# Gathering the seven products of w_up and w_down in shared PSUM tiles, forming the activation sums in the up stage, and 30 instead of 22 column blocks of w_down as sevens

## The chip, the cores and the metric

The kernel runs on one core of a Trainium2 chip. Times are device microseconds (us) of one execution. Before the change three runs took 2043.04, 2046.28 and 2048.93 us; the median is 2046.28 us. Engines are named as in the profile: PE is TensorE, PEld its weight loads, DVE VectorE, ACT ScalarE, POOL GpSimd, SP the engine that issues most DMAs.

## The reference, cut to what matters

A decoder layer on 512 tokens with 16 meta tokens in front: RMSNorm, one input projection, windowed attention beside an mLSTM, an output projection with residual; then the part that the change touches, a squared-ReLU MLP with D_MODEL = 2048 and D_FF = 8192, and a final norm.

```python
u = rmsnorm(h, norm_mlp[l])
h = h + jnp.square(jax.nn.relu(u @ w_up[l])) @ w_down[l]
...
h = rmsnorm(h, norm_final)
```

## The kernel before, in words

All large products are float32 work done as three passes of TensorE: each operand is split into a high part (a ScalarE copy that rounds to float32r, L116) and a low part (a VectorE subtraction, L117), and hi x hi, hi x lo and lo x hi are added up in PSUM. `split` (L115) does one operand; `hi_lo` (L122) gives weight operands from three rotating pairs of tiles `whi`, `wlo` of 128 x 1024. So a weight operand can be made at most two products ahead of TensorE: the third waits until a product has freed its pair.

The MLP is stored and multiplied as 2 x 2 blocks with Winograd's seven products in place of eight. Three stages follow each other.

**Output projection** (up to 711 us). It makes the operands of the seven products for w_up, `yh` and `yl` for p = 0 to 6, partly in pool b2 in the order of `ORDER` (L44), partly in the slots s0 to s31 (`xslot`).

**Up stage** (711 to 1354 us). 32 quads, `up_quad` (L734). A quad loads two raw tiles of 1 MB with blocks x11, x12, x22, x21, forms four sums s1 to s4 on VectorE (`w_sum`, L731, 128 x 1024 each), makes seven weight operands and runs seven products of 24 matmuls with 256 columns (L754 to 756). The products go into four PSUM tiles of their own (pa, pb, pc, pd; odd quads use the second set of four banks). When all are done they are gathered: a copy of the first (L795) and five VectorE adds (L796 to L800) give the four result blocks `d`; Relu and Square on ScalarE (L803, L804) and one store of 512 KB on ACT's queue into `fdram[quad]` (L805) follow. The last quad does it on VectorE and POOL's queue.

**Down stage** (1354 us to the end). The 8192 rows are cut into NC = 8 chunks; each chunk has four column blocks of 512. The activations of a chunk come back from `fdram` (`f_load`, L935: 512 KB a load), and are split into units (`f_unit`, L922): four plain ones, f = 0, 1, 7, 3, and four of sums, f = 2, 4, 5, 6, for which `f_sums` (L950) first does four VectorE operations of 128 x 512 per pair. Plain units are double buffered (slots for even chunks, tiles r for odd ones), the slots of the sums are single: a chunk's sums can only be written once the chunk before has used its own. A column block is done in one of two ways:

- `down_seven` (L997): two raw loads of 1 MB with y11|y21 and y22|y12, four sums, seven products of 24 matmuls with 256 columns (L1012 to 1014) in seven PSUM tiles, then a copy (L1031) and six VectorE adds (L1036 to L1042) into d.
- `down_classic` (L978): two raw loads, four weight operands, 96 matmuls with 512 columns (L706 to 708) from the plain units alone.

`add_block` (L967) and `classic_done` (L991) scale each quarter on ScalarE and add it to `hd` in memory with an accumulating DMA on POOL's queue. Blocks 0 and 1 of each chunk and block 2 of chunks 1 to 6 are sevens, 22 in all; block 3, and block 2 of chunks 0 and 7, are classic, 10 in all, the very last of them token by token with the final norm (after L1091). In each chunk the plain units of the next one are prepared behind its second seven, and the sums while its classic block runs (L1053 to L1066). Raw loads rotate through two `raw_tile`s and one tile of pool b3f (`raw3`, L962).

The order on each engine and queue is not written out: the program is built with `schedule_with_timeline_sim=True` (L1203), where a planner orders the instructions by the place in the program and by when it holds their inputs and tiles to be ready; each engine then runs its queue in that order, and semaphores for tiles and PSUM banks are added by the framework.

Of the kernel before, what the change touches and what calls it, by code (L numbers as in the profile page):

```python
# [10 lines left out]
F32 = mybir.dt.float32  # L11
# [32 lines left out]
ORDER = (0, 1, 3, 4, 6, 5, 2)  # L44
# [38 lines left out]
def hybrid_layer(ctx, tc, io, out):  # L83
# [98 lines left out]
    groups = [(0, 1), (1, 1)] + [(k, 2) for k in range(2, KT, 2)]  # L182
    with tc.tile_pool(name="a0", bufs=1) as a0:
# [511 lines left out]
    fdram = [dpool.tile([P, 4 * HTOK], F32, name=f"fd{i}") for i in range(NQ)]  # L695
# [38 lines left out]
    def up_quad(quad):  # L734
# [12 lines left out]
        pa, pb, pc = (nb((P, 2, HTOK)) for _ in range(3))  # L747
        pd = nb((P, HTOK))

        def product(p, w, out, q0=0, q1=KQ):  # L750
            for q in range(q0, q1):
                wh, wl = (t[:, q * P : (q + 1) * P] for t in w)
                ah_, al_ = yh[p, q // 2][:, q % 2], yl[p, q // 2][:, q % 2]
                pe.matmul(out, wh, ah_, start=q == 0, stop=False)  # L754
                pe.matmul(out, wh, al_, start=False, stop=False)  # L755
                pe.matmul(out, wl, ah_, start=False, stop=q == KQ - 1)  # L756

        pp2, pp6 = pa[:, 1], pd[:]
        if quad == 0:
            pp2, pp6 = pp6, pp2  # L760
# [16 lines left out]
            product(5, operand(s2[:]), pp6)  # L777
        else:
            product(0, operand(x11), pa[:, 0])
            product(1, operand(x12), pp2)  # L780
            product(3, operand(x22), pc[:, 0])
            w_sum(s1, x21, x22, ALU.add)
            w_sum(s2, s1[:], x11, ALU.subtract)
            product(4, operand(s1[:]), pb[:, 1])
            w_sum(s3, x11, x21, ALU.subtract)
            product(6, operand(s3[:]), pb[:, 0])
            w_sum(s4, x12, s2[:], ALU.subtract)
            product(5, operand(s2[:]), pp6)
            product(2, operand(s4[:]), pc[:, 1])

        d = b2b.tile([P, 4, HTOK], F32, name="d", bufs=2)
        sb = b2b.tile([P, HTOK], F32, name="sb")
        u2 = b2b.tile([P, 1, HTOK], F32, name="u2")
        u = b2b.tile([P, 2, HTOK], F32, name="u")
# [412 lines left out]
```

## Time and profile before

| what | before |
|---|---|
| median of 3 runs | 2046.28 us (2043.04 to 2048.93) |
| span of the profiled execution | 2042.5 us |
| median less span | 3.8 us |
| TensorE busy, matmuls | 2010.7 us, 14208 |
| VectorE, ScalarE busy | 1425.2 us, 964.5 us |
| DMA traffic | 284.44 MB, mean 139 GB/s |

The profiler gives the span of its one execution, 2042.5 us, and no other time for it; what lies around the span is taken as the median of the runs less the span. In the tables by stretch, a row has the stretch, its length, the busy time and count of PE, PEld, DVE, ACT and POOL, the granted TensorE clock as a share of full speed, the mean busy share of the 16 DMA engines, and GB/s. In the groups of instructions a row has line, engine, operation, tiles out<-in, shapes and count, then busy us and mean ns of one, then the engine's idle time before them with what ended it. In the waits a row has who waited for whom, us in total, times and the longest.

### The profile page before, as it was taken

How to read it: one execution, taken by the hardware profiler on the slowest of the kernel's cores; microseconds unless marked ns; L12 is line 12 of the kernel's file. 1: busy time of each engine (PE TensorE's matmuls, PEld its weight loads, DVE VectorE, ACT ScalarE, POOL GpSimd, SP SyncE). 2: the span in 40 equal slices, each digit the busy share in tenths (PEclk: the TensorE clock that was granted, in tenths of full speed). 3: DMA queues.
4: the chain of work that ended last, by engine and by line, in shares of the span. 5: the costliest groups of instructions: out<-in, count | busy, mean ns of one | idle time of the engine just before them, and what ended most of it. 6: DMA issues, size and time to landing. Idle time of an engine off the chain costs nothing.

```text
span 2042.5 us, 34088 instructions
## 1 busy us (share of the span) xinstructions
PE 2010.7 (98%) x14208; PEld 1865.8 (91%) x14208; DVE 1425.2 (70%) x1916; ACT 964.5 (47%) x1378; POOL 198.3 (10%) x295
## 2 busy tenths in 40 slices
PE   9999999999999999999999999999999999999998
PEld 7878889988888899999999999988989999899996
DVE  6556763233544587778777877779787897988874
ACT  4433542244433454444444444445555555655553
POOL 0111220012120000000000000001211111211200
PEclk9999999999999999999999999999999999999999
DMA  7412122211433353434334343436665866756762
GB/s 306 137 54 85 63 65 102 83 62 64 139 128 130 118 182 108 155 106 153 119 141 136 123 154 105 155 136 194 176 175 133 218 179 173 180 152 185 196 205 95
DMA packets 72507, 284.44 MB, mean 139 GB/s; under 512 B 11520, under 2 KB 15744, under 8 KB 49168
## 3 DMA queue, kind: packets, MB, share of 16 engines
q1 hardware_dynamic: 50032, 232.96, 33.1%
q0 software_dynamic: 16560, 30.94, 9.2%
q10 hardware_dynamic: 5760, 18.36, 2.2%
q8 instruction: 111, 1.82, 0.4%
q14 instruction: 44, 0.36, 0.1%
HBM read 227.67 MB, written 54.56 MB: 138 GB/s over the span
## 4 chain that ended last, share of the span: by engine, by line
PE 86%; DVE 5%; DMA 5%; ACT 2%; issue 1%; POOL 0%; DVEq 0%; POOLq 0%; SPq 0%; ACTq 0%
PE g L163 10%; PE a L754 5%; PE a L756 5%; PE a L755 5%; PE g L754 5%; PE g L756 5%; PE g L755 5%; PE g L706 4%; PE g L708 4%; PE g L707 4%; DMA raw<-in_w4w_dram 4%; PE g L1013 2%; PE g L1014 2%; PE g L178 2%; PE g L225 2%; PE g L1012 2%
## 5 line engine op out<-in xcount | busy, mean ns | idle before, releaser
L116 ACT CAST whi<-raw 128x1024 fp32r<-128x1024 f32 x294 | 308.5, 1050 | 525.1 <-PE g L708 120.7
L117 DVE TENSOR_TENSOR wlo<-raw,whi 128x1024 fp32r<-128x1024 f32 x294 | 359.4, 1223 | 198.0 <-ACT whi L116 192.5
L117 DVE TENSOR_TENSOR wlo<-s,whi 128x1024 fp32r<-128x1024 f32 x216 | 263.9, 1224 | 106.6 <-ACT whi L116 106.2
L116 ACT CAST whi<-s 128x1024 fp32r<-128x1024 f32 x216 | 226.3, 1048 | 235.3 <-PE a L755 75.3
L163 PE MATMUL g<-s,whi 128*128 128x264 f32 x1216 | 205.0, 287 | 0.2 <-DVE qa L261 0.2
L163 PEld LDWEIGHTS g<-s,whi 128*128 128x128 f32 x1216 | 170.9, 189 | 5.4 <-issue 4.9
L1012 PE MATMUL g<-whi,s 128*128 128x256 f32 x496 | 137.6, 279 | 2.7 <-ACT whi L116 2.7
L1013 PE MATMUL g<-wlo,s 128*128 128x256 f32 x496 | 138.8, 281 | 1.1 <-DVE wlo L117 1.1
L1013 PE MATMUL a<-wlo,s 128*128 128x256 f32 x472 | 132.7, 282 | 6.7 <-DVE wlo L117 6.7
L1014 PE MATMUL g<-whi,s 128*128 128x256 f32 x496 | 138.6, 280 | 0.0
L707 PE MATMUL g<-wlo,s 128*128 128x512 f32 x352 | 138.4, 393 | 0.0
L708 PE MATMUL g<-whi,s 128*128 128x512 f32 x352 | 138.1, 395 | 0.0
L706 PE MATMUL g<-whi,s 128*128 128x512 f32 x352 | 136.7, 396 | 0.1
L1014 PE MATMUL a<-whi,s 128*128 128x256 f32 x472 | 131.8, 280 | 0.0
L1012 PE MATMUL a<-whi,s 128*128 128x256 f32 x472 | 130.5, 280 | 1.1 <-ACT whi L116 1.1
L163 PE MATMUL g<-s,wlo 128*128 128x264 f32 x608 | 128.0, 287 | 0.0
L754 PE MATMUL g<-yh,whi 128*128 128x256 f32 x448 | 126.6, 283 | 1.1 <-ACT whi L116 1.1
L756 PE MATMUL a<-yh,wlo 128*128 128x256 f32 x448 | 126.4, 282 | 0.6 <-DVE wlo L117 0.6
L756 PE MATMUL g<-yh,wlo 128*128 128x256 f32 x448 | 126.3, 282 | 0.0
L754 PE MATMUL a<-yh,whi 128*128 128x256 f32 x448 | 126.3, 282 | 0.0
L754 PE MATMUL a<-s,whi 128*128 128x256 f32 x448 | 126.2, 282 | 0.0
L755 PE MATMUL g<-yl,whi 128*128 128x256 f32 x448 | 126.1, 282 | 0.0
(375 smaller groups left out, 5640.4 us busy)
## 6 DMA issues: line engine op xcount, KB each, us to landing
raw<-in_w_dram SPq DMA_DIRECT2D x112, 1024.0 KB, 5.4
raw<-in_w4w_dram SPq DMA_DIRECT2D x44, 1024.0 KB, 6.8
hd<-d POOLq DMA_DIRECT2D x112, 256.0 KB, 7.9
raw<-in_w4c_dram SPq DMA_DIRECT2D x20, 1024.0 KB, 6.6
fd<-d ACTq DMA_DIRECT2D x31, 512.0 KB, 6.5
fr<-fd SPq DMA_DIRECT2D x28, 512.0 KB, 4.9
xtok<-in_x_dram SPq DMA_DIRECT2D x4, 1024.0 KB, 11.3
hs<-in_x_dram SPq DMA_DIRECT2D x16, 256.0 KB, 6.4
```

The costliest lines, as they stand in the source:

```text
L116: act.copy(dst_hi, src)
L117: dve.tensor_tensor(out=dst_lo, in0=src, in1=dst_hi.bitcast(F32), op=ALU.subtract)
L163: pe.matmul(ps[s][:], w, x[:, s * HALF : (s + 1) * HALF], start=first and kt == 0, stop=last and kt == KT - 1,)
L706: pe.matmul(ps[b][:], a, wh, start=kt == first, stop=False)
L707: pe.matmul(ps[b][:], a, wl, start=False, stop=False)
L708: pe.matmul(ps[b][:], c, wh, start=False, stop=kt == last)
L754: pe.matmul(out, wh, ah_, start=q == 0, stop=False)
L755: pe.matmul(out, wh, al_, start=False, stop=False)
L756: pe.matmul(out, wl, ah_, start=False, stop=q == KQ - 1)
L1012: pe.matmul(ps[p][:, t], a, wh[:, cols], start=q == 0, stop=False)
L1013: pe.matmul(ps[p][:, t], a, wl[:, cols], start=False, stop=False)
L1014: pe.matmul(ps[p][:, t], a2, wh[:, cols], start=False, stop=q == FQ - 1)
```

## The change

The first quad still gathers from four PSUM tiles. Every other quad of the up stage uses three accumulators in two PSUM tiles: X, and W and Q in one bank. Product 0 goes into X and is copied out by ScalarE; products 5, 6 and 3 are added to X in turn, with a copy of X ("snapshot") after 5 and after 6; 1 goes into W, 4 into Q, is copied, and 2 is added to Q. Three VectorE adds finish the blocks. The products run in the order 0, 1, 5, 4, 6, 2, 3, and ORDER follows it. After Square, four more VectorE operations form the sums of the activations, and two stores of 512 KB per quad go out on ACT's queue, with 1 KB pieces side by side for a pair of quads.

In the down stage `f_load`, `f_plain` and `f_sums` are gone: each unit is loaded by itself (256 KB, SP's queue, five buffers `fu`) and split; unit 7 is loaded for chunks 0 and 7 alone. The sevens use X, W and Q in three banks in the same way. All blocks but (chunk 0, block 3) and the last one are sevens. The raw tiles hold y11|y12 and y21|y22, and pool b3f has two raw buffers. The next chunk's plain units 0, 1, 3 are prepared behind block 1, its sums behind block 3. The input arrays `w4c` and `w4w` are laid out to match.

```diff
-ORDER = (0, 1, 3, 4, 6, 5, 2)
+ORDER = (0, 1, 5, 4, 6, 2, 3)
...
+    fdram = [[dpool.tile([P, 4, 2, HTOK], F32, name=f"fd{i}_{n}") for n in range(2)] for i in range(NQ // 2)]
...
+        def product(p, w, out, q0=0, q1=KQ, start=True):
             for q in range(q0, q1):
                 wh, wl = (t[:, q * P : (q + 1) * P] for t in w)
                 ah_, al_ = yh[p, q // 2][:, q % 2], yl[p, q // 2][:, q % 2]
-                pe.matmul(out, wh, ah_, start=q == 0, stop=False)
-                pe.matmul(out, wh, al_, start=False, stop=False)
-                pe.matmul(out, wl, ah_, start=False, stop=q == KQ - 1)
-
-        pp2, pp6 = pa[:, 1], pd[:]
+                pe.matmul(out, wh, ah_, start=start and q == 0, stop=False, skip_group_check=True)
+                pe.matmul(out, wh, al_, start=False, stop=False, skip_group_check=True)
+                pe.matmul(out, wl, ah_, start=False, stop=q == KQ - 1, skip_group_check=True)
...
+            X, B = nb((P, HTOK)), nb((P, 2, HTOK))
+            W, Q = B[:, 0], B[:, 1]
+            d = b2b.tile([P, 4, HTOK], F32, name="d", bufs=2)
+            product(0, operand(x11), X[:])
+            act.copy(d[:, 0], X[:])
             w_sum(s1, x21, x22, ALU.add)
             w_sum(s2, s1[:], x11, ALU.subtract)
+            product(1, operand(x12), W)
+            product(5, operand(s2[:]), X[:], start=False)
+            dve.tensor_tensor(out=d[:, 0], in0=d[:, 0], in1=W, op=ALU.add)
+            act.copy(d[:, 2], X[:])
+            product(4, operand(s1[:]), Q)
             w_sum(s3, x11, x21, ALU.subtract)
+            act.copy(d[:, 1], Q)
+            product(6, operand(s3[:]), X[:], start=False)
             w_sum(s4, x12, s2[:], ALU.subtract)
+            act.copy(d[:, 3], X[:])
+            product(2, operand(s4[:]), Q, start=False)
+            dve.tensor_tensor(out=d[:, 3], in0=d[:, 3], in1=d[:, 1], op=ALU.add)
+            act.activation(d[:, 0], d[:, 0], AF.Relu)
+            product(3, operand(x22), X[:], start=False)
+            dve.tensor_tensor(out=d[:, 2], in0=d[:, 2], in1=Q, op=ALU.add)
+            act.activation(d[:, 2:4], d[:, 2:4], AF.Relu)
+            act.activation(d[:, 1], X[:], AF.Relu)
+        act.activation(d[:], d[:], AF.Square)
+        fs = b2b.tile([P, 4, HTOK], F32, name="fs")
+        dve.tensor_tensor(out=fs[:, 0], in0=d[:, 2], in1=d[:, 3], op=ALU.add)
+        dve.tensor_tensor(out=fs[:, 1], in0=fs[:, 0], in1=d[:, 0], op=ALU.subtract)
+        dve.tensor_tensor(out=fs[:, 2], in0=d[:, 2], in1=d[:, 0], op=ALU.subtract)
+        dve.tensor_tensor(out=fs[:, 3], in0=d[:, 1], in1=fs[:, 1], op=ALU.subtract)
+        act.dma_start(out=fdram[quad // 2][0][:, :, quad % 2], in_=d[:])
+        act.dma_start(out=fdram[quad // 2][1][:, :, quad % 2], in_=fs[:])
...
-        split(hi[:], lo[:], src)
...
-    def f_sums(c, pair):
-        a11, a12, a21, a22 = (frs[c, pair][:, :, i] for i in range(4))
-        s1, s2 = (b3.tile([P, 2, HTOK], F32, name=f"fs{i}")[:] for i in range(2))
-        dve.tensor_tensor(out=s1, in0=a21, in1=a22, op=ALU.add)
-        dve.tensor_tensor(out=s2, in0=s1, in1=a11, op=ALU.subtract)
-        dve.tensor_tensor(out=a12, in0=a12, in1=s2, op=ALU.subtract)
-        dve.tensor_tensor(out=a21, in0=a11, in1=a21, op=ALU.subtract)
-        for f, src in ((2, a12), (4, s1), (5, s2), (6, a21)):
-            f_unit(c, pair, f, src)
...
+        pos = FPOS.index(f)
+        fu = b3f.tile([P, 2, HTOK], F32, name="fu", bufs=5)
+        sync.dma_start(out=fu[:], in_=fdram[2 * c + pair][pos // 4][:, pos % 4])
+        split(hi[:], lo[:], fu[:])
+
+    def prepare(c, fs):
+        for f in fs:
+            for pair in range(2):
+                f_unit(c, pair, f)
 
     raws_ = iter(range(1, 1 << 20))
 
     def raw3(src):
-        raw = raw_tile() if next(raws_) % 3 < 2 else b3f.tile([P, 2048], F32, name="raw3")
+        raw = raw_tile() if next(raws_) % 4 < 2 else b3f.tile([P, 2048], F32, name="raw3", bufs=2)
...
+        y11, y12 = raws[0][:, :1024], raws[0][:, 1024:]
+        y21, y22 = raws[1][:, :1024], raws[1][:, 1024:]
...
+        X, W, Q = bank((P, 2, HTOK)), abank((P, 2, HTOK)), abank((P, 2, HTOK))
+        d = b3.tile([P, NB, 512], F32, name="d", bufs=2)
+
+        def product(p, w, out, start=True):
...
+                    last = t == 1 and q == FQ - 1
+                    pe.matmul(out[:, t], a, wh[:, cols], start=start and t == q == 0, stop=False, skip_group_check=True)
+                    pe.matmul(out[:, t], a, wl[:, cols], start=False, stop=False, skip_group_check=True)
+                    pe.matmul(out[:, t], a2, wh[:, cols], start=False, stop=last, skip_group_check=True)
+
+        def c_out(row, col):
+            return d[:, 2 * row : 2 * row + 2, col * HTOK : (col + 1) * HTOK]
+
+        product(0, operand(y11), X)
+        act.copy(c_out(0, 0), X[:])
         w_sum(t1, y12, y11, ALU.subtract)
         w_sum(t2, y22, t1[:], ALU.subtract)
+        product(1, operand(y21), W)
+        product(5, operand(t2[:]), X, start=False)
+        dve.tensor_tensor(out=c_out(0, 0), in0=c_out(0, 0), in1=W[:], op=ALU.add)
+        act.copy(c_out(0, 1), X[:])
+        w_sum(t3, y12, y22, ALU.subtract)
+        product(4, operand(t1[:]), Q)
+        act.copy(c_out(1, 0), Q[:])
         w_sum(t4, y21, t2[:], ALU.subtract)
+        product(6, operand(t3[:]), X, start=False)
+        act.copy(c_out(1, 1), X[:])
+        product(2, operand(y22), Q, start=False)
+        dve.tensor_tensor(out=c_out(1, 1), in0=c_out(1, 1), in1=c_out(1, 0), op=ALU.add)
+        product(3, operand(t4[:]), X, start=False)
+        dve.tensor_tensor(out=c_out(0, 1), in0=c_out(0, 1), in1=Q[:], op=ALU.add)
+        act.copy(c_out(1, 0), X[:])
...
-    prepare(0, f_plain)
+    prepare(0, PLAIN)
+    down_classic(0, 3, classic_done)
+    prepare(0, (5, 4, 6, 2))
     for c in range(NC - 1):
-        if c == 0:
-            down_classic(c, 3, classic_done)
-            prepare(c, f_sums)
-        down_seven(c, 0, add_block)
-        down_seven(c, 1, add_block)
-        prepare(c + 1, f_plain)
-        if c == 0:
-            down_classic(c, 2, classic_done)
-        else:
-            down_seven(c, 2, add_block)
-            down_classic(c, 3, classic_done)
-        prepare(c + 1, f_sums)
+        for j in range(3 if c == 0 else 4):
+            down_seven(c, j, add_block)
+            if j == 1:
+                prepare(c + 1, (0, 1, 3))
+        prepare(c + 1, (5, 4, 6, 2))
+        if c == NC - 2:
+            prepare(c + 1, (7,))
...
-    down_classic(c, 2, last_done)
+    down_seven(c, 2, last_done)
```

## Rows read from the trace of the kernel before

**Rows 1.** The page's first part: span; busy time by engine.

```profile
span 2042.5 us, 34088 instructions
...
PE 2010.7 (98%) x14208; PEld 1865.8 (91%) x14208; DVE 1425.2 (70%) x1916; ACT 964.5 (47%) x1378; POOL 198.3 (10%) x295
```

**Rows 2.** Busy time by stretch: up stage, then three stretches of the down stage.

```profile
771.00:1334.00 563.00, 563.00 (x4738) 563.00 (x4737) 444.98 (x455) 268.93 (x283) 0.00 (x0) 1.00 0.38 132
1354.20:1445.30 91.10, 85.38 (x530) 75.83 (x529) 81.65 (x104) 52.06 (x74) 11.87 (x14) 1.00 0.63 179
...
1697.40:1781.50 84.10, 81.50 (x602) 77.10 (x602) 70.66 (x83) 46.73 (x61) 13.95 (x17) 1.00 0.67 176
...
1476.00:1496.00 20.00, 16.96 (x130) 16.75 (x129) 13.97 (x16) 7.21 (x9) 0.57 (x1) 0.91 0.42 117
```

**Rows 3.** Timeline of PE at four borders between classic blocks and sevens.

```profile
1593.91 0.63 PE L706 MATMUL a<-whi,s 128*128 128x512 f32 x2
...
1616.12 0.40 PE L1012 MATMUL g<-whi,r 128*128 128x256 f32 x2
...
1675.66 0.63 PE L706 MATMUL a<-whi,r 128*128 128x512 f32 x2
...
1697.44 0.40 PE L1012 MATMUL g<-whi,s 128*128 128x256 f32 x2
```

**Rows 4.** Waits of PE in the down stage, 1354.2 to 2043 us.

```profile
PE a L1013 <- DVE wlo L117: 9.7, 7, 3.0
PE g L1013 <- DVE wlo L117: 3.4, 4, 1.6
PE g L1012 <- ACT whi L116: 2.7, 1, 2.7
PE a L1012 <- ACT whi L116: 1.1, 1, 1.1
```

**Rows 5.** The chain that ended last, 1465 to 1490 us: start us, us, what.

```profile
1474.69 8.34 DMA raw<-in_w4w_dram
...
1487.25 1.15 DVE wlo L117
```

**Rows 6.** Groups of instructions by shape, DVE, 1400 to 1990 us.

```profile
L117 DVE TENSOR_TENSOR wlo<-raw,whi 128x1024 fp32r<-128x1024 f32 x93 | 113.3, 1220 | 17.7 <-ACT whi L116 17.4
...
L732 DVE TENSOR_TENSOR s<-raw,s 128x1024 f32<-128x1024 f32 x42 | 51.3, 1221 | 0.4
L117 DVE TENSOR_TENSOR s<-fr,s 128x512 fp32r<-128x512 f32 x52 | 35.1, 686 | 5.0 <-ACT s L116 5.0
...
L953 DVE TENSOR_TENSOR fs<-fr 128x512 f32<-128x512 f32 x13 | 8.9, 686 | 0.1
...
L1036 DVE TENSOR_TENSOR d<-sb,g 128x512 f32<-128x512 f32 x11 | 7.5, 680 | 0.0
```

**Rows 7.** Groups of instructions by shape, ACT, 1400 to 1990 us.

```profile
L116 ACT CAST whi<-raw 128x1024 fp32r<-128x1024 f32 x92 | 96.7, 1052 | 120.4 <-PE a L1014 41.9 <-PE g L1014 35.8 <-PE g L708 23.5
...
L969 ACT ACTIVATE d<-d,r 128x512 f32<-128x512 f32 x80 | 52.8, 715 | 22.8 <-DVE d L1042 18.7 <-DVE d L1040 4.1
L116 ACT CAST s<-fr 128x512 fp32r<-128x512 f32 x52 | 31.9, 619 | 17.5 <-DMA fr<-fd 4.4 <-PE g L1013 3.6 <-DVE fr L955 3.6
...
L1031 ACT COPY sb<-g 128x512 f32<-128x512 f32 x11 | 6.4, 578 | 0.0
```

**Rows 8.** Waits in the up stage, 771 to 1334 us.

```profile
ACT whi L116 <- PE a L755: 145.8, 84, 1.8
ACT whi L116 <- PE g L755: 144.4, 83, 2.0
```

**Rows 9.** Groups of instructions by shape in the up stage, ACT and DVE.

```profile
L795 ACT COPY sb<-g 128x256 f32<-128x256 f32 x14 | 5.1, 363 | 0.0
...
L796 DVE TENSOR_TENSOR d<-sb,g 128x256 f32<-128x256 f32 x14 | 5.8, 414 | 0.0
```

**Rows 10.** The page's DMA issues: count, KB each, us to landing.

```profile
fd<-d ACTq DMA_DIRECT2D x31, 512.0 KB, 6.5
```

More of the change, by code (lines that the diff above doesn't have):

```diff
@@ L694, in hybrid_layer @@
     hd = [[dpool.tile([P, 512], F32, name=f"hd{j}_{b}") for b in range(NB)] for j in range(NJ)]
-    fdram = [dpool.tile([P, 4 * HTOK], F32, name=f"fd{i}") for i in range(NQ)]
+    NC = 8
+    fdram = [[dpool.tile([P, 4, 2, HTOK], F32, name=f"fd{i}_{n}") for n in range(2)] for i in range(NQ // 2)]
     ssh = cpool.tile([P, NB, NJ], F32, name="ssh")
@@ L777, in up_quad @@
             product(5, operand(s2[:]), pp6)
-        else:
-            product(0, operand(x11), pa[:, 0])
-            product(1, operand(x12), pp2)
-            product(3, operand(x22), pc[:, 0])
+            d = b2b.tile([P, 4, HTOK], F32, name="d", bufs=2)
+            v = b2b.tile([P, 4, HTOK], F32, name="fs")
+            sb, u2, u = v[:, 2], v[:, 3], v[:, :2]
+            act.copy(sb, pa[:, 0])
+            dve.tensor_tensor(out=d[:, 0], in0=sb, in1=pp2, op=ALU.add)
+            dve.tensor_tensor(out=u2, in0=sb, in1=pp6, op=ALU.add)
@@ new lines, in up_quad @@
+            dve.tensor_tensor(out=u, in0=v[:, 3:].to_broadcast([P, 2, HTOK]), in1=pb[:], op=ALU.add)
+            dve.tensor_tensor(out=d[:, 3], in0=u[:, 0], in1=pb[:, 1], op=ALU.add)
+            dve.tensor_tensor(out=d[:, 1:3], in0=u, in1=pc[:], op=ALU.add)
+            act.activation(d[:], d[:], AF.Relu)
+        else:
+            X, B = nb((P, HTOK)), nb((P, 2, HTOK))
+            W, Q = B[:, 0], B[:, 1]
+            d = b2b.tile([P, 4, HTOK], F32, name="d", bufs=2)
+            product(0, operand(x11), X[:])
+            act.copy(d[:, 0], X[:])
@@ L787, in up_quad @@
+            product(6, operand(s3[:]), X[:], start=False)
             w_sum(s4, x12, s2[:], ALU.subtract)
[L788 to L794, printed above, removed]
-        act.copy(sb[:], pa[:, 0])
-        dve.tensor_tensor(out=d[:, 0], in0=sb[:], in1=pp2, op=ALU.add)
@@ L1022, in down_seven @@
-        w_sum(t3, y22, y12, ALU.subtract)
-        product(5, operand(t2[:]))
-        w_sum(t4, y21, t2[:], ALU.subtract)
-        product(6, operand(t3[:]))
-        product(3, operand(t4[:]))
-        d = b3.tile([P, NB, 512], F32, name="d", bufs=2)
-        sb = b3.tile([P, 2, HTOK], F32, name="sb")
-        u0, u1 = (b3.tile([P, 2, HTOK], F32, name=f"u{i}") for i in range(2))
-        act.copy(sb[:], ps[0][:])
-        def c_out(row, col):
-            return d[:, 2 * row : 2 * row + 2, col * HTOK : (col + 1) * HTOK]
```

80 lines of the change are left out of this document (13 added, 67 removed).

## The prediction

> **What bounds the kernel now.** I read the page first: TensorE is busy for 2010.7 us of a span of 2042.5 us, so only what shortens its stream or its gaps can move the end [rows 1]. A busy share of matmuls says little about their pace, so I read paces next, in the table by stretch. In the up stage 4738 matmuls of 256 columns fill 563 us without a gap, 0.119 us each, with the full clock granted; VectorE is busy for 79% of it and ScalarE for 48% [rows 2]. In the down stage the timeline gives clean blocks: a classic block of 96 matmuls of 512 columns runs from 1593.91 to 1616.12 (22.21 us), the next from 1675.66 to 1697.44 (21.78 us), and the 504 matmuls between, three sevens, take 59.54 us, 19.85 us each [rows 3]. So a seven is 2.15 us shorter than a classic block (mean 22.0 us), and one product of 24 matmuls lasts 2.84 us.
>
> Third, the waits. In the up stage before, TensorE waits for nothing. In the down stage it waits 16.9 us in all: 13.1 us for the low half of a weight operand, 3.8 us for a high half [rows 4]. The chain shows what stands behind them: a load of w_down lands late, VectorE forms the sums and the low half late, TensorE idles [rows 5]. VectorE is the busy helper there (70.66 of 84.1 us in one chunk of the down stage, 84%, against 46.73 us for ScalarE) [rows 2].
>
> **The change part by part.** The sum is made against the profiled span of 2042.5 us. The median of the runs is 3.8 us longer (2046.28 us); I add that at the end.
>
> *Eight more blocks as sevens.* Before, 10 of 32 blocks of w_down are classic (one of them the token by token end); afterwards 2. 8 x (22.0 - 19.85) = **-17.2 us**, on TensorE itself, so nothing hides it; this term is only lost if a wait eats it. [...]
>
> *Four raw buffers, and other halves side by side.* A load of w_down now has two b3f buffers beside the two raw tiles (before one), and a pair holds y11|y12 and y21|y22, so the first sum needs the first load alone. The waits with the chain of rows 5 should go: two whole blocks fit, and a load can start 20 us ahead, where it took 8.34 us and came late. Bounds: -16.9 us (all TensorE waits) and 0. I take **-8 us**, about half, because VectorE stays nearly full, as follows.
>
> *VectorE in the down stage.* A seven has 7 low halves and 4 sums of 1.22 us, and 6 adds of 0.68 us; afterwards 3 such adds. Per chunk before: 3 x 17.5 + a classic block's 4 low halves (4.9) + 16 unit splits (11.0) + 8 sum operations (5.5) = 73.9 us, against 59.55 + 22.0 = 81.6 us of TensorE. Afterwards: 4 x 15.5 + 14 x 0.687 = 71.6 us against 4 x 19.85 = 79.4 us [rows 6]. So 90% as before; the sum operations leave, but the classic block, in which VectorE caught up, leaves too. What used to be done under it (the splits of the activation sums, whose slots are single) must now follow the products: each pair of slots comes free when the last seven of the chunk has used it and is needed seven products later, six products or 17 us of cover. Cost 0; if that cover goes, each late pair is 2 x 0.69 us on the path.
>
> *Snapshots.* One PSUM tile X now takes products 0, 5, 6 and 3 in turn, with a ScalarE copy after each of the first three; a second (Q) takes 4 and then 2. Each copy must finish within the one product between: 2.84 us. No row shows such a copy between two products; the nearest are the copies at the end of a seven, 0.363 us (256 columns) and 0.578 us (512) [rows 7, 9]. In front of one can stand a weight cast of 1.05 us that is already running: 1.6 us together, inside 2.84. In the up stage ScalarE waits for TensorE 290 us of 563 [rows 8], so it is free when a product ends: cost 0; the cover is that wait. There W and Q also share one bank, so product 4 waits for VectorE's add of W; product 5 lies between. In the down stage ScalarE rises from 3 x 10.8 + 7.1 + 9.9 = 49.4 us a chunk to 4 x (7.35 + 2.89 + 2.86) + 14 x 0.618 = 61.0 us of 79.4 (60% to 77%) [rows 7]. In the last seven of a chunk, copy, weight cast and two unit casts make 2.87 us against 2.84, and the product with two scalings as well 3.7. That is about 1.1 us late per chunk, 7.7 us over seven chunks if no operand made ahead absorbs it; I take half, **+4 us**. Bounds 0 (a copy cannot shorten the stream) and the price under the second rival.
>
> *Activation sums in the up stage.* Per quad VectorE has four adds of 256 columns more (0.41 us each [rows 9]) and two of 512 fewer (0.69 us [rows 6]), 15.8 to about 16.1 us of 20; ScalarE gains three copies and a Relu in three pieces, 1.5 us, to 11 of 20. TensorE waits for neither now [rows 2], so nothing can be gained. One store of 512 KB more per quad, issued by ScalarE behind VectorE's last subtraction: what is queued behind it are weight casts, which run two products ahead, and it lands in about 6.5 us [rows 10] of the 20 us that its single tile has. The stretch's DMA share rises from 0.38 to some 0.46. Cost 0; the upper bound is ScalarE's extra work on the path, 1.5 us x 31 quads = 46 us, which needs its 290 us of waiting gone, and is counted with the second rival. On SP's queue, 30 reads of 512 KB become 116 of 256 KB, ahead of or behind weight loads; a chunk then moves about 206 GB/s against 176, share 0.78 against 0.67 [rows 2]. Cost 0 as long as four raw buffers keep loads a block ahead. POOL's queue loses its three transfers and keeps the accumulating stores.
>
> *The end.* The last seven (7,2) stands where a classic block left the slots of the sums free for 22 us. Now the eight splits of the last weights (0.62 + 0.69 us each) follow that block's products, the last two pairs one product before use: 0 to 8 x 0.69 = 5.5 us, **+2 us**. The start of the stage keeps its classic block as cover; 0.
>
> Sum: -17.2 - 8 + 4 + 2 = -19.2 us; 2023.3 us of span, **2027 us** of time.
>
> **The rivals.** *All waits go.* The extra raw buffer is all that was missing, as three sevens in a row without a wait suggest [rows 3]: -17.2 - 16.9 = -34 us, 2012 us. Against it: VectorE at 90%.
>
> *A late snapshot, the slower end.* In the down stage a copy is queued behind a weight cast that itself waits for the end of the product between, or for a sum that VectorE has not formed. Then TensorE idles for that cast and the copy, 1.05 + 0.58 = 1.63 us. There are 4 such places in each of 61 sevens. If one in every seven of the down stage is late, 30 x 1.63 = 49 us: 2027 + 49 = **2076 us**. It decides from 12 late copies on (19.2 / 1.63) of 244. For it: each engine runs its queue in order, the order is a planner's and not the source's, and ScalarE has at most 2.84 us. Against: the copy stands earlier in the program than the casts it competes with, and those wait for the same product's end. [...] The clock would join in only at longer waits: a stretch with one of 3.0 us was granted 0.91, the start of the stage with waits up to 2.7 us 1.00 [rows 2, 4].
>
> *VectorE becomes the bound.* If a chunk keeps the 84.1 us that one takes now [rows 2], because VectorE's idle share (16%) stays whatever the blocks are, the shorter stream turns into waits: 71.6 / 0.84 = 85 us a chunk, **2046 us**, no change. For: 90%. Against: part of the idle time is the load wait that goes.
>
> **How the numbers follow.** Forecast (2014 to 2040) 0.65, all waits go 0.10, VectorE bound 0.09, late snapshots 0.16. About 0.3% (6 us) is what a measurement tells from no change, so faster 0.75, same 0.09, slower 0.16. The range 2008 to 2052 takes in the first three and the lightest of the fourth (a late copy in half of the down sevens gives 2051).
>
> **What would show it.** Right: 5040 matmuls of the sevens at about 0.118 us; no TensorE wait in the up stage; fewer waits for low halves with w_down loads behind them; a chunk near 80 us. Wrong: TensorE waits whose releaser is a ScalarE copy out of X or Q, repeated per seven; a chunk above 82 us; a gap before the last columns above 5 us; an up stage longer than 20 us a quad.

## The result, and the profile after

The changed kernel takes 2033.14 us (median; 2032.67 to 2035.11) against 2045.14 us for the kernel before on the same chip: a ratio of 0.9938, 95% interval 0.9923 to 0.9953, so 12.0 us faster. The profiled execution spans 2033.3 us against 2042.5. The forecast was 2027 us, in a range of 2008 to 2052.

In the code after, the up products are L753 to L755, the classic ones L707 to L709, the sevens L1009 to L1011. ScalarE's snapshots are L1017 (X after product 0), L1023 (X after 5), L1026 (Q after 4) and L1029 (X after 6), the last copy L1034, the scalings by r2 L964; a unit is loaded at L947 and cast at L116.

First the page's busy times, to set against [rows 1]:

```profile
span 2033.3 us, 35953 instructions
...
PE 1993.5 (98%) x14784; PEld 1878.7 (92%) x14784; DVE 1397.5 (69%) x1897; ACT 1083.4 (53%) x1675; POOL 199.5 (10%) x292
```

The table by stretch (columns as in [rows 2]): the up stage, the first classic block with the wait ahead of it, its first part alone, and chunks 1 to 6 from the first matmul of chunk 1 to that of chunk 7.

```profile
771.00:1334.00 563.00, 563.00 (x4738) 563.00 (x4738) 435.63 (x508) 301.97 (x422) 0.00 (x0) 1.00 0.46 158
...
1357.20:1383.80 26.60, 24.44 (x100) 19.27 (x99) 18.23 (x25) 13.58 (x21) 0.00 (x0) 0.94 0.86 274
...
1357.20:1365.00 7.80, 5.64 (x18) 4.03 (x17) 5.58 (x10) 5.09 (x8) 0.00 (x0) 0.78 0.86 292
...
1446.40:1938.00 491.60, 476.85 (x4034) 474.62 (x4034) 402.07 (x420) 339.35 (x468) 84.74 (x96) 1.00 0.79 205
```

The up stage holds the same 4738 matmuls in the same 563 us. Ahead of that stretch, in the second quad, TensorE has four waits, with L800 the add of W:

```profile
PE a L753 <- DVE d L800: 0.8, 1, 0.8
PE a L753 <- ACT whi L116: 0.6, 2, 0.3
PE a L755 <- DVE wlo L117: 0.6, 1, 0.6
```

Chunks 1 to 6 are 24 sevens, 24 x 19.85 = 476.4 us at the pace of [rows 3]; they take 491.6, so 15.2 us are lost there. What is lost, the waits of PE from 1357 us to the end show, against [rows 4]:

```profile
PE g L1009 <- ACT d L1017: 16.9, 8, 2.8
PE g L1009 <- ACT d L1029: 2.8, 5, 0.6
PE g L707 <- ACT s L116: 2.1, 1, 2.1
PE g L1009 <- ACT d L989: 0.4, 1, 0.4
```

In the down stage no wait for a low half (DVE wlo) or a weight cast (ACT whi) is left. In their place product 5 waits for the snapshot of product 0, once in the first seven of each of the eight chunks. The timeline of ACT at such a border (start, us, what, idle before), and the matmul that waited, in the timeline of PE:

```profile
1447.44 1.97 ACT L116 CAST s<-fu 128x512 fp32r<-128x512 f32 x3 [2.46 <-DMA fu<-fd]
1449.32 0.58 ACT L1034 COPY d<-g 128x512 f32<-128x512 f32 x1
1449.80 1.05 ACT L116 CAST whi<-s 128x1024 fp32r<-128x1024 f32 x1
1450.75 0.62 ACT L116 CAST s<-fu 128x512 fp32r<-128x512 f32 x1
1451.27 2.57 ACT L964 ACTIVATE d<-d,r 128x512 f32<-128x512 f32 x4
1453.73 0.61 ACT L116 CAST s<-fu 128x512 fp32r<-128x512 f32 x1
1454.24 0.58 ACT L1017 COPY d<-g 128x512 f32<-128x512 f32 x1
```

```profile
1454.88 0.39 PE L1009 MATMUL g<-whi,s 128*128 128x256 f32 x1 [2.51 <-ACT d L1017]
```

ScalarE first stands 2.46 us for a unit's landing, then works off what piled up: five unit casts, a copy, a weight cast and four scalings stand ahead of the snapshot. Eight sum-unit casts of the next chunk, and six plain casts of the chunk after it, all come here: fourteen in some 25 us (at the last border it is the eight and two of unit 7). Plain units have slots of their own and are not needed for 80 us; the planner puts them ahead of their place in the source, where they stand behind block 1 of the next chunk.

### The profile page after: what moved, and what is told of

The parts are those of the page before. It is cut to its first block, busy times and chain, and to the rows that moved or that the text cites. A ratio compares the mean times of both kernels' runs of the same rounds, so it can differ in the third digit from the quotient of the medians.

```text
span 2033.3 us, 35953 instructions
## 1 busy us (share of the span) xinstructions
PE 1993.5 (98%) x14784; PEld 1878.7 (92%) x14784; DVE 1397.5 (69%) x1897; ACT 1083.4 (53%) x1675; POOL 199.5 (10%) x292
## 4 chain that ended last, share of the span: by engine, by line
PE 89%; DMA 4%; ACT 3%; DVE 3%; issue 1%; POOL 1%; POOLq 0%; DVEq 0%; ACTq 0%
PE g L163 9%; PE a L753 5%; PE a L755 5%; PE g L753 5%; PE g L755 5%; PE a L754 5%; PE g L754 5%; PE g L1009 5%; PE g L1011 5%; PE g L1010 5%; DMA fu<-fd 3%; PE a L1010 3%; PE a L1011 3%; PE a L1009 3%; PE g L707 3%; PE g L709 3%
## 5 line engine op out<-in xcount | busy, mean ns | idle before, releaser
L116 ACT CAST whi<-raw 128x1024 fp32r<-128x1024 f32 x286 | 300.9, 1052 | 406.4 <-PE g L709 91.3
L117 DVE TENSOR_TENSOR wlo<-raw,whi 128x1024 fp32r<-128x1024 f32 x286 | 350.0, 1224 | 207.1 <-ACT whi L116 201.7
L117 DVE TENSOR_TENSOR wlo<-s,whi 128x1024 fp32r<-128x1024 f32 x248 | 302.4, 1223 | 140.8 <-ACT whi L116 137.7
L116 ACT CAST whi<-s 128x1024 fp32r<-128x1024 f32 x248 | 260.8, 1053 | 157.0 <-PE g L754 64.5
L1009 PE MATMUL g<-whi,s 128*128 128x256 f32 x720 | 201.5, 280 | 18.9 <-ACT d L1017 16.9
L1010 PE MATMUL g<-wlo,s 128*128 128x256 f32 x720 | 201.6, 280 | 0.0
L1011 PE MATMUL g<-whi,s 128*128 128x256 f32 x720 | 201.4, 280 | 0.0
L1010 PE MATMUL a<-wlo,s 128*128 128x256 f32 x600 | 167.6, 279 | 0.0
L1011 PE MATMUL a<-whi,s 128*128 128x256 f32 x600 | 167.6, 279 | 0.0
L1009 PE MATMUL a<-whi,s 128*128 128x256 f32 x600 | 166.7, 278 | 0.0
L1009 PEld LDWEIGHTS g<-whi,s 128*128 128x128 f32 x720 | 135.0, 188 | 21.3 <-ACT d L1017 18.5
L965 POOL DMA_DIRECT2D hd<-d x108 | 95.3, 1115 | 461.9 <-ACT d L964 461.9
L1011 PEld LDWEIGHTS g<-whi,s 128*128 128x128 f32 x720 | 136.5, 190 | 0.0
L1010 PEld LDWEIGHTS g<-wlo,s 128*128 128x128 f32 x720 | 135.2, 188 | 0.0
L753 PE MATMUL a<-yh,whi 128*128 128x256 f32 x448 | 126.5, 282 | 1.5 <-DVE d L800 0.8
L753 PE MATMUL g<-yh,whi 128*128 128x256 f32 x448 | 126.6, 282 | 1.1 <-ACT whi L116 1.1
L755 PE MATMUL a<-yh,wlo 128*128 128x256 f32 x448 | 126.4, 282 | 0.6 <-DVE wlo L117 0.6
L755 PE MATMUL g<-yh,wlo 128*128 128x256 f32 x448 | 126.2, 282 | 0.0
L753 PE MATMUL a<-s,whi 128*128 128x256 f32 x448 | 126.1, 282 | 0.0
```

The lines of the kernel that those rows point to most:

```text
L116: act.copy(dst_hi, src)
L117: dve.tensor_tensor(out=dst_lo, in0=src, in1=dst_hi.bitcast(F32), op=ALU.subtract)
L753: pe.matmul(out, wh, ah_, start=start and q == 0, stop=False, skip_group_check=True)
L755: pe.matmul(out, wl, ah_, start=False, stop=q == KQ - 1, skip_group_check=True)
L965: pool.dma_start(out=hd[j][b][:], in_=d[:, b], accum_op=ALU.add)
L1009: pe.matmul(out[:, t], a, wh[:, cols], start=start and t == q == 0, stop=False, skip_group_check=True)
```

## The experiments

Each time is a median with the ratio to the kernel before on the same chip. "Chunks 1 to 6" is, for each run, the stretch from the first matmul of chunk 1 to that of chunk 7: the same 4032 matmuls, 476.4 us without a loss.

**Why the snapshot is late: landing, queue order, or the snapshot itself.** The first four runs: three try a remedy that turns out wrong, the fourth undoes the gather. nf (the weights of the final norm) moves into a raw3 tile where the added tiles need its place.

```diff
# e1_fu9
-        fu = b3f.tile([P, 2, HTOK], F32, name="fu", bufs=5)
+        fu = b3f.tile([P, 2, HTOK], F32, name="fu", bufs=9)
...
-    nf = b3f.tile([P, D], F32, name="nf")[:]
+    nf = b3f.tile([P, 2048], F32, name="raw3", bufs=2)[:]
```

> Nine buffers fu for unit loads instead of five (the final norm weights take a raw tile to make room; chunk 7 then has three raw tiles). Theory L, landing: the late copy after product 0 at the head of each chunk (eight TensorE waits, 16.9 us) starts with ScalarE idle in front of a unit cast whose load could not be issued for want of a buffer; with nine the cast never waits for DMA, ScalarE is 2 to 3 us earlier, at least six of the eight waits go, and the time is 2017 to 2023 us against 2033. Theory Q, queue: the copy is late because four scalings and unit casts stand in front of it; the waits shrink only by what the DMA wait was, and 2026 to 2031 us remain. Theory F, ScalarE simply full: no change, 2031 to 2035 us.

Measured: 2048.99 us, ratio 1.0008 (0.9999 to 1.0018), some 15 us slower than the change and above all three ranges. Chunks 1 to 6 take 504.0 us. The waits of PE in the down stage, and the timeline of ACT at the border:

```profile
PE g L1009 <- ACT d L1023: 9.7, 6, 2.7
PE g L1009 <- ACT d L1017: 6.9, 5, 1.7
PE g L1009 <- ACT whi L116: 4.5, 6, 1.7
PE g L1010 <- DVE wlo L117: 3.8, 6, 0.8
```

```profile
1434.08 1.66 ACT L116 CAST s<-fu 128x512 fp32r<-128x512 f32 x3 [4.05 <-DMA fu<-fd]
...
1439.55 2.18 ACT L116 CAST s<-fu 128x512 fp32r<-128x512 f32 x4
```

With more buffers the planner puts more casts in a row, at the borders up to four where the change has up to three, and they still run into a landing: more buffers did not take the landing away. What makes this kernel slower than the change was not isolated; 12.4 of the 15 us are lost in chunks 1 to 6, and 3.3 in chunk 7 (65.3 us against 62.0), where nf holds a raw buffer.

```diff
# e2_defer
         product(0, operand(y11), X)
         act.copy(c_out(0, 0), X[:])
+        flush()
...
-        done(c, j, d)
+        held.append((done, c, j, d))
...
```

> The four scalings and stores of a seven are written down behind the next seven's first copy, everything else as in the change. Theory Q: the planner now puts the copy after product 0 in front of the scalings, the eight waits go and the time is 2015 to 2021 us. Theory L: the copy still stands behind a unit cast that waits for its load; waits shrink by the 2.6 us of the scalings where the load lands in time and stay where it does not, 2020 to 2029 us. Theory F: the scalings are done later and some other copy is late instead, 2031 to 2035 us.

Measured: 2034.82 us, ratio 0.9947 (0.9934 to 0.9960), the change's own time. The trace is of an execution of 2041.5 us. The scalings are written behind the next seven's snapshot, but ScalarE's timeline still has the four of them ahead of it, at 1453.62 us (the snapshot, now L1024, runs at 1456.59): the planner's order is not the source's. So this run does not test what the scalings cost. The wait stays:

```profile
PE g L1016 <- ACT d L1024: 16.3, 7, 3.0
```

e3_both makes both edits.

> Both edits: nine unit buffers, and the scalings written behind the next seven's first copy. Theories L and Q: no snapshot wait above 1 us is left, 2013 to 2020 us; if one of the two alone was the cause, the same time as that run within 3 us. Theory F: TensorE still waits for ScalarE about 15 us in the down stage, 2028 us or more.

Measured: 2051.49 us, ratio 1.0016 (1.0003 to 1.0030): like e1_fu9.

```diff
# e4_banks: the gather undone, one of seven banks for each product
-        product(0, operand(y11), X)
-        act.copy(c_out(0, 0), X[:])
+        product(0, operand(y11))
...
+        act.copy(sb[:], ps[0][:])
+        dve.tensor_tensor(out=c_out(0, 0), in0=sb[:], in1=ps[1][:], op=ALU.add)
...
```

> The sevens of w_down gather as before the change, seven PSUM tiles, one copy and six VectorE adds at the end; up stage, stored sums, four raw buffers and 30 sevens stay (the final norm weights take a raw tile). Theory S: the waits are the price of the snapshots, so the eight waits on the copy vanish; VectorE gets 3 x 0.68 us more a seven, 8 us a chunk on 67, still under 80, so the time is 2015 to 2024 us. Rival V: without the snapshots VectorE is the bound again; TensorE waits for low halves at the head of each chunk come back with 1 to 3 us each, and the time is 2028 to 2040 us.

Measured: 2043.61 us, ratio 0.9985 (0.9976 to 0.9994), above both ranges; chunks 1 to 6 take 493.9 us against 491.6, chunk 7 69.3 against 62.0. With no snapshot to wait for, TensorE waits for the same ScalarE elsewhere, at a weight cast:

```profile
PE g L1008 <- ACT whi L116: 13.6, 8, 4.3
PE a L1008 <- ACT whi L116: 3.6, 3, 1.7
PE g L1009 <- DVE wlo L117: 2.4, 4, 1.0
```

The longest of these, 4.3 us, lies in chunk 7 and has another cause, the place of nf (below, at e13_banks_spread). In chunks 1 to 6 as much is lost as with snapshots, so the wait is not the price of reading one bank between two products. ScalarE is late at the border, and whatever comes next on it is what TensorE waits for. That gave a new theory: it is the fourteen casts in one place, each stopping ScalarE until its load lands.

**Taking the burst apart.** Each plain unit of the next chunk gets a block of its own (0, 1 and 3 in blocks 0, 1 and 2). An order edge keeps its load behind that block's raw load, and its casts behind that block's snapshot of Q.

```diff
# e11_spread3
-            if j == 1:
-                prepare(c + 1, (0, 1, 3))
+            if j < 3:
+                with tc.issue_after(gate["sp"].ins), tc.issue_after(gate["act"].ins):
+                    prepare(c + 1, ((0, 1, 3)[j],))
```

> Only where plain-unit casts and loads stand is changed: each of the three plain units of the next chunk is prepared in a block of its own and queued behind that block's raw load on SP and behind its snapshot of Q on ScalarE, so that six of the fourteen casts and loads leave the chunk's border. Theory B (ScalarE is late at the border because fourteen casts in a row wait there for their landings): the eight waits behind the snapshot of product 0 (16.9 us with the changed kernel) fall under 5 us together and the five behind the snapshot after product 6 stay at 2.8 us or under; span 2016 to 2022, time 2018 to 2023. Rival A (the eight sum casts, which stay at the border, are enough to make it late): waits of 1.5 to 2.1 us remain at each border, time 2029 to 2034. Rival L2 (the in-chunk loads land late and stop ScalarE there): new waits within the chunks, time 2033 or more.

Measured: 2027.7 us, ratio 0.9906 (0.9891 to 0.9921). The waits of PE from 1350 us on, and the timeline of ACT at a border:

```profile
PE a L1012 <- DVE wlo L117: 2.8, 6, 0.5
PE g L1011 <- ACT d L1019: 2.5, 2, 1.6
...
PE g L1011 <- ACT d L1031: 1.4, 1, 1.4
```

```profile
1608.43 0.62 ACT L116 CAST s<-fu 128x512 fp32r<-128x512 f32 x1 [1.78 <-DMA fu<-fd]
1608.96 0.58 ACT L1036 COPY d<-g 128x512 f32<-128x512 f32 x1
1609.44 1.05 ACT L116 CAST whi<-s 128x1024 fp32r<-128x1024 f32 x1
1610.38 2.56 ACT L966 ACTIVATE d<-d,r 128x512 f32<-128x512 f32 x4
1612.85 0.57 ACT L1019 COPY d<-g 128x512 f32<-128x512 f32 x1
```

The snapshot of product 0 (now L1019) is waited for twice and 2.5 us in place of eight times and 16.9. A landing still stops ScalarE, and the four scalings still stand ahead of the snapshot; with one cast to catch up on, it is in time. Chunks 1 to 6 take 485.1 us. Theory B holds on the waits (the edit moves the loads of these units off the border too, and does not tell casts from loads); the time came out 4.7 us over its upper end: 8.7 us are still lost in chunks 1 to 6, and chunk 7, whose unit 7 is still cast at the last border, gained nothing (63.8 us against 62.0).

```diff
# e9_pool
-            act.activation(d[:, b], d[:, b], AF.Copy, scale=r2[:, b : b + 1])
+            pool.tensor_scalar(out=d[:, b], in0=d[:, b], scalar1=r2[:, b : b + 1], scalar2=1.0, op0=ALU.mult, op1=ALU.mult)
```

> The four scalings by r2 of each seven go from ScalarE (2.57 us a block) to GpSimd, whose queue holds only the stores that follow them; the casts stay where they are. Theory F (ScalarE has too much to do around a border, whatever it is): with 2.6 us less ahead of the snapshot of product 0 its waits of 2.1 us go; time 2016 to 2022. Theory B (casts that wait for landings): ScalarE stands at a landing, not for want of time, so about half of each wait stays; time 2024 to 2031. Against both: GpSimd's work costs VectorE or the stores something, and the time is 2033 or more.

Measured: 2030.08 us, ratio 0.9917 (0.9900 to 0.9935); waits behind the first snapshot 2.2 us, behind the one after product 6 4.3 us, chunks 1 to 6 486.0 us. The time lies in theory B's range and above theory F's, but nearly all of the first snapshot's waits went, where B let half of them stay. So theory F's cure works as well: taking 2.6 us of other work off the border does what taking six casts off it does, and the two theories are one (what ScalarE has to do there, the standing still included, must fit).

**Both cures, and the last border.** e14_best has e11's and e9's edits and casts unit 7 of the last chunk within chunk 6's last block, behind that block's snapshot of Q.

```diff
# e14_best, on e11_spread3 and e9_pool
-            if j < 3:
+            if j < 3 or c == NC - 2:
...
-                    prepare(c + 1, ((0, 1, 3)[j],))
+                    prepare(c + 1, ((0, 1, 3, 7)[j],))
...
-        if c == NC - 2:
-            prepare(c + 1, (7,))
```

> Both cures together: plain units spread over the blocks as in e11_spread3, scalings on GpSimd as in e9_pool, and plain unit 7 of the last chunk cast in mid-chunk 6 in place of the last border (where e11 still waits 5.0 us, at 1924 to 1937). If what is left at the borders is ScalarE's work, the two savings add in part: e11 has 11.4 us of gaps in the down stage, of which the last border's 5.0 and about half of the rest go: span 2018 to 2022, time 2019 to 2024. If they are the same saving taken twice: e11's time, 2026 to 2029. If GpSimd's scaling comes late for the two result tiles: over 2030.

Measured: **2018.79 us**, ratio 0.9858 (0.9843 to 0.9873), faster than both kernels. One wait above 1 us behind a copy is left, with the landing that makes it (waits of PE; timeline of ACT), and chunk 7 runs without a gap (table by stretch):

```profile
PE g L1011 <- ACT d L1031: 4.5, 1, 4.5
```

```profile
1919.01 0.62 ACT L116 CAST s<-fu 128x512 fp32r<-128x512 f32 x1 [4.24 <-DMA fu<-fd]
```

```profile
1445.70:1926.80 481.10, 476.04 (x4035) 475.63 (x4034) 416.96 (x425) 282.22 (x375) 208.53 (x192) 1.00 0.83 211
...
1926.80:1986.40 59.60, 59.60 (x507) 59.60 (x506) 57.59 (x67) 38.18 (x60) 6.22 (x8) 1.00 0.40 116
```

Chunks 1 to 6 take 481.1 us, 4.7 above no loss at all; chunk 7's three sevens take 59.60 us, 3 x 19.85 = 59.55. Of e11's loss there (8.7 us) and e9's (9.6), about half came off again: against the change e11 saves 6.5 us in chunks 1 to 6, e9 5.6, both together 10.5, so the savings add for the most part. In chunk 7 e9_pool, which leaves unit 7 at the last border, takes 59.6 us as well, so what the third edit is worth is not shown.

**What the eight further sevens are worth.**

```diff
# e6_classic: block 3 of chunks 1 to 6 classic again, 24 sevens of 32 blocks
-            down_seven(c, j, add_block)
+            if j == 3:
+                down_classic(c, 3, classic_done)
+            else:
+                down_seven(c, j, add_block)
             if j == 1:
-                prepare(c + 1, (0, 1, 3))
+                prepare(c + 1, (0, 1, 7, 3))
...
```

> The fourth block of chunks 1 to 6 is a classic product again (24 of the 32 blocks are sevens, against 30), with a fourth plain unit cast in mid-chunk; the gather stays. Term one of my sum (a classic block is 2.15 us longer on TensorE): 6 x 2.15 = 12.9 us slower than the changed kernel if the border waits stay, time about 2046. Rival W (the eight sum units can be cast during the classic block, which needs none of them and no snapshots, so the border waits of 2.1 us go): 12.9 - 6 x 2.1 = 0.3 us, time about 2033.

Measured: 2032.38 us, ratio 0.9927 (0.9910 to 0.9943): no slower than the change, though TensorE's stream is 6 x 2.15 = 12.9 us longer. The waits of PE say why:

```profile
PE g L1009 <- ACT d L1017: 3.3, 2, 1.7
```

Rival W holds. A classic block at the end of a chunk has no snapshots and uses none of the sum units; under it ScalarE finishes the casts in time, and the eight border waits become two. What six of the eight sevens save on TensorE, the change loses again at its borders.

**Where the old waits went.** The waits of [rows 4] are gone wholly, where I had counted on half. Four parts of the change could have done it: the fourth raw buffer, the halves side by side, the sums off VectorE, the gather. Each was undone, the others kept (the pairing on e5_raw1, so with three buffers; the sums and the gather on e11_spread3, where the border waits that could cover an effect are mostly gone).

```diff
# e5_raw1
-        raw = raw_tile() if next(raws_) % 4 < 2 else b3f.tile([P, 2048], F32, name="raw3", bufs=2)
+        raw = raw_tile() if next(raws_) % 3 < 2 else b3f.tile([P, 2048], F32, name="raw3")
```

> One buffer less for the weights: three in place of four, as in the kernel before; all else as changed. Theory T (the term of my sum: the waits for late low halves and casts went because loads come earlier): some 8 us of waits for whi and wlo come back; time 2038 to 2045. Rival U (they went because a seven's recombination is shorter on VectorE and its last bank is read alone, and the loads were early enough): no new waits; time 2032 to 2036.

Measured: 2037.62 us, ratio 0.9959 (0.9943 to 0.9974), an interval that overlaps the change's. No wait for a low half or a weight cast comes back in the down stage; the waits are those of the change (first snapshot 15.5 us, after product 6 3.4 us). The time lies between the two expectations, the trace is rival U's: with the new pairing the fourth buffer is not needed to keep the old waits away. Four buffers with the old pairing were not tried.

```diff
# e17_pairs, on e5_raw1 (and w4w packed to match)
-        y11, y12 = raws[0][:, :1024], raws[0][:, 1024:]
-        y21, y22 = raws[1][:, :1024], raws[1][:, 1024:]
+        y11, y21 = raws[0][:, :1024], raws[0][:, 1024:]
+        y22, y12 = raws[1][:, :1024], raws[1][:, 1024:]
```

> e5_raw1 (three raw buffers) with the operand halves in the loads as in the kernel before: y11 and y21 in the first, y22 and y12 in the second, so that the first sum needs both loads and both are held until late in the block. Theory H (the pairing is what brought the next loads forward: each buffer is free earlier): VectorE's waits for a landing of raw come back (35.4 us in the kernel before, none in e5), and with them 5 to 15 us of waits on TensorE; time 2042 to 2052. Rival J (with the sums gone from VectorE and the snapshots in place the loads have room in either pairing): e5's time within 3 us, 2034 to 2041; then neither the buffer, the pairing, the sums nor the gather alone explains the old waits.

Measured: 2054.60 us, ratio 1.0046 (1.0030 to 1.0062): 17 us above e5_raw1 and slower than the kernel before, from nothing but which half lies beside which. The waits of PE, of DVE and of SP's queue in the down stage:

```profile
PE g L1009 <- ACT d L1017: 10.2, 6, 6.1
PE a L1010 <- DVE wlo L117: 9.8, 11, 2.2
PE g L1009 <- ACT d L1023: 6.7, 6, 1.4
```

```profile
DVE s L733 <- DMA raw<-in_w4w_dram: 21.9, 15, 3.1
```

```profile
SPq L959 <- DVE s L733: 336.0, 26, 19.8
```

In the kernel before the line that answers to the second is this one, and e5_raw1 has none:

```profile
DVE s L732 <- DMA raw<-in_w4w_dram: 35.4, 14, 4.1
```

The late low halves are back (9.8 us of PE's waits, as the 9.7 of [rows 4]), and so is VectorE's wait for a load. SP's raw loads now wait for a sum to release the buffer, up to 19.8 us, where in e5_raw1 most wait for a low half, up to 14.3. With y21 in the first load and y12 in the second, the first sum needs both loads, and the first load is held until t4 where it was t3; which of the two weighs more was not separated. Theory H holds, the time 2.6 us beyond its range. The kernel before with the new pairing alone was not tried.

```diff
# e16_sums, on e11_spread3
+        if f in SUMS:
+            dve.tensor_tensor(out=fu[:], in0=fu[:], in1=fu[:], op=ALU.max)
         split(hi[:], lo[:], fu[:])
```

> e11_spread3 with eight VectorE instructions of 128x512 f32 per chunk put back, one ahead of the cast of each sum unit (the maximum of the loaded tile with itself, in place: the values stay), as many and of the size that the kernel before spends on forming the sums there (0.69 us each). Theory D (the old waits for late low halves went because the sums left VectorE in the down stage): waits for whi, wlo and unit casts come back, 8 to 20 us, time 2035 to 2048. Rival G (they went through the gather, which has two recombining adds fewer and reads its banks one at a time): under 3 us more than e11, time 2027 to 2031.

Measured: 2026.09 us, ratio 0.9891 (0.9876 to 0.9906), against e11's 2027.7. VectorE is busy 429.9 us of chunks 1 to 6 in place of 401.1, and the time as a whole is no longer. Chunks 1 to 6 take 487.8 us in place of 485.1, with one wait of 0.9 us for a weight cast in each where e11 has 0.5 for a low half; chunk 7 takes 60.1 in place of 63.8. The waits for whi and wlo make 8.7 us against e11's 4.5, where theory D has 8 to 20 us come back. Moving the sums into the up stage is not what removed the old waits.

```diff
# e13_banks_spread: e4_banks' edits on e11_spread3, the casts queued behind the copy of product 0 (here at the block's end)
-        act.copy(sb[:], ps[0][:])
+        gate["act"] = act.copy(sb[:], ps[0][:])
```

> e11_spread3 with the gather undone: seven banks a block, one copy and six adds behind the last product (and nf in the raw3 tile, as in e4_banks). Theory P (with the border spread, a snapshot costs nothing and the old recombination nothing either: neither is the bound): within 4 us of e11, time 2024 to 2032. Theory S (the snapshots are what costs): faster than e11 by its 3.9 us of waits behind snapshots, 2022 to 2025. Theory V (the six adds on VectorE are what the change rightly removed): low halves late at the block's ends, 0.3 to 0.7 us for each of 30 blocks, time 2035 to 2048.

Measured: 2039.56 us, ratio 0.9954 (0.9937 to 0.9970). The number is theory V's, but its mechanism is not in the trace: late low halves make 0.6 us, weight casts 18.1. The table by stretch, chunks 1 to 6 and chunk 7, and the timeline of ACT in chunk 7:

```profile
1449.90:1936.30 486.40, 478.80 (x4034) 476.65 (x4033) 453.37 (x515) 289.94 (x371) 84.53 (x96) 1.00 0.80 206
1936.30:2008.20 71.90, 63.98 (x507) 62.59 (x506) 61.28 (x76) 34.63 (x53) 3.54 (x4) 0.95 0.38 112
```

```profile
1962.03 1.99 ACT L116 CAST whi<-raw 128x1024 fp32r<-128x1024 f32 x2 [11.19 <-DMA raw<-in_w4w_dram]
```

Over 24 sevens the old gather takes 486.4 us and the snapshots of e11 485.1: no difference worth the name, with VectorE at 93% in the one and 83% in the other. What this kernel loses against e11 lies outside: 4.9 us in the three sevens of chunk 0 (64.6 us against 59.7, with one wait of 2.9 us for a weight cast behind a unit's landing), 8.1 in chunk 7 (71.9 against 63.8). The longest wait of chunk 7, 5.0 us, is for the weight cast of the row above, ahead of which ScalarE stands 11.2 us for a load of w_down: a late load, not the old gather on VectorE. Here nf holds a raw buffer, and the chunk's loads take turns on three; e4_banks, with the same nf, has the same wait (10.4 us of ScalarE, 4.3 of TensorE). e1_fu9 has nf there too, with snapshots and without that long wait of TensorE, and takes 65.3 us for chunk 7; which share is nf's and which the banks' was not tried.

## Why the prediction was right

It was right in sign, and 6.1 us under the measured 2033.1. The sum was -19.2 us of span; measured are -9.2. From the last matmul of the up stage to the last of all TensorE took 2032.92 - 1354.05 = 678.9 us before and 2022.00 - 1357.17 = 664.8 after. Blocks at 19.85 and 22.0 us make 656.7 and 639.5 of that, so 17.2 came off the stream, and the loss went from 22.2 to 25.3: other waits, not fewer. The rest of the 9.2 is an up stage that ends 3.1 us later and a tail 1.7 us longer. The nearness to the forecast is in part luck: two terms were wrong by much and in opposite ways, the old waits (16.9 us gone, 8 forecast) and the snapshots (19.7 us lost, 4 forecast). By its terms:

- **Eight more blocks as sevens, -17.2.** The stream of TensorE did shorten by that: sevens kept their pace (chunk 7 of e14_best, 19.87 us each). By e6_classic what six of the eight give is taken away again at the borders, so in this kernel they are worth nothing measurable. In e14_best, with 4.7 us lost in chunks 1 to 6, the shorter stream should count; a classic block was not put back there.
- **Four raw buffers and other halves, -8.** All the waits of [rows 4] went: the -16.9 that I had as the bound. I took half because VectorE was nearly full. That was the wrong reason: with VectorE at 93% chunks 1 to 6 take 1.3 us more than at 83% (e13_banks_spread), and eight more VectorE instructions a chunk do not lengthen the run (e16_sums). Of the two edits that I lumped together, the pairing carries it (17 us, e17_pairs against e5_raw1, with three buffers) and the fourth buffer, with the new pairing, 4.5 us between medians whose intervals overlap.
- **Snapshots, +4.** This step failed in size: 16.9 + 2.8 = 19.7 us of waits. The place was nearly right (copy, weight cast and unit casts in one product; not in a chunk's last seven but in the first of the next). But I counted two unit casts of 0.62 us a product, 1.1 us late per chunk, halved. (The 3.7 us there is a slip: with two scalings of 0.715 us the 2.87 become 4.3, and the product 1.5 us late.) The planner adds the six plain casts of the chunk after next to the eight of the sums, and ScalarE stands for their landings, which my sum of busy times leaves out: 2.1 us a border. That it is the burst and not the snapshot, e11_spread3 (the 16.9 become 2.5) and e4_banks (as much lost over chunks 1 to 6, without snapshots) show.
- **VectorE, cost 0**, and **sums in the up stage, cost 0.** Right, VectorE 435.6 us of 563 against 445.0 in [rows 2] and no wait of TensorE there. But the up stage ended 3.1 us later, 0.9 of it ahead of its first matmul and the rest in its first two quads by PE's timeline. In the second quad the four waits shown with the result make 2.0 us, against one of 0.6 before; the longest, 0.8 us, is for the add that frees the bank of W and Q, which VectorE does behind the first quad's old gather; the prediction put that wait at nothing because product 5 lies between. It comes once in 31 quads, and no run looked into it.
- **The end, +2.** The last columns begin without a gap; only the tail behind the last matmul is 1.7 us longer (11.3 against 9.6), which no run looked into.
- **The start, 0.** Wrong by 4 us: the first classic block waits 2.1 us for a unit's cast (the wait at L707) and then takes 24.2 us (1359.59 to 1383.79) where [rows 3] have 22.0.

Of the rivals, the late snapshot came in its light form: 13 late copies, about the 12 from which I had it decide, at 1.5 us each, though by another queue than the rival has, unit casts that stand for their landings and not a weight cast that waits for a product or a sum; the old waits that went as well kept the sign. VectorE as the bound is refuted. Nor does the loss lie in X being one bank: with a bank for each product the time was no better (e4_banks 2043.6 us, e13_banks_spread 2039.6, both with nf moved), and chunks 1 to 6 took as long (493.9 us against 491.6, and 486.4 against e11's 485.1).

## What to carry to other kernels

Before adding a buffer, look at which operands share a load and which of them is read last: the next load into that buffer waits for that reader (in e5_raw1 up to 14.3 us for a low half, in e17_pairs up to 19.8 for a sum). When an engine that copies between two products also prepares later operands, add up its queue at the place where preparations meet, with the landings that it will stand for, and not its mean share; then put what has a slot of its own and time in hand elsewhere. A gain on the busiest engine is collected only where the helpers' bursts leave room (here 2033.1 us with six sevens that shorten TensorE's stream by 12.9, 2032.4 without them), so measure the parts one by one.

## What the runs showed of the hardware that was not expected

GpSimd's scalings slowed VectorE's low halves. In e9_pool a scaling takes 1448 ns on GpSimd, against 2.57 us for four on ScalarE; the groups from 1454 to 1940 us, of e9_pool and then of the change:

```profile
L964 POOL TENSOR_SCALAR d<-d,r 128x512 f32<-128x512 f32 x97 | 127.9, 1448 | 285.4 <-DVE d L1033 185.4 <-ACT d L1034 100.0
...
L117 DVE TENSOR_TENSOR wlo<-s,whi 128x1024 fp32r<-128x1024 f32 x97 | 127.6, 1315 | 57.5 <-ACT whi L116 57.4
```

```profile
L117 DVE TENSOR_TENSOR wlo<-s,whi 128x1024 fp32r<-128x1024 f32 x95 | 115.5, 1222 | 57.8 <-ACT whi L116 57.6
```

The same low half takes 1315 ns in place of 1222. VectorE's work in chunks 1 to 6 rises from 402.1 us to 419.3: 17 us for 96 scalings, 0.18 us each. In e9_pool's trace the 33 of 96 such low halves that started while a scaling ran took 1490 ns on average, the others 1211 to 1220; the six adds with an operand in PSUM that started during one took 674 ns, no longer than the 683 and 677 of their groups. Why a scaling makes a low half longer and such an add not was not shown. VectorE, busy for 419.3 of the 486.0 us of those chunks, had the time to give.

The clock: over the 7.8 us from 1357.2 to 1365 us, which begin with the first classic block's wait of 2.1 us, the granted clock is 0.78. From 1361.66 to 1364.22 us the block's matmuls start 0.43 us apart, from 1365.24 us on 0.23, and the block takes 24.2 us where [rows 3] have 22. Waits as long or longer at the chunk borders (up to 2.8 us, at 1393 us) are followed by a clock of 1.00 (1393.5 to 1400 us). So the prediction's sentence that the clock joins in only at longer waits did not hold: the length of a wait alone does not tell, and what else does stays open.
